# Feed-forward products by Strassen's scheme over pairs of tiles, its sums on GpSimd, in a float32 streaming encoder

## The chip, the cores and the metric

One NeuronCore of a Trainium2 chip runs the program. The metric is device microseconds (us) of one execution; a lower number is better. TensorE is PE in the rows below, VectorE DVE, ScalarE ACT, GpSimd POOL, and SyncE, which issues most transfers, SP.

## What is computed

A trunk of two layers over 528 tokens (16 meta tokens and 512 frames) with 1024 features: first a multi-scale retention layer, then a layer of latent attention; each ends with a dense feed-forward network (FFN) of hidden width 2816. Cut to what matters here:

```python
def swiglu(hn, w1, w3, w2):
    return (jax.nn.silu(hn @ w1) * (hn @ w3)) @ w2

for layer in range(2):
    h = h + mixer(rmsnorm(h, norm_mix_g[layer]))
    h = h + swiglu(rmsnorm(h, norm_ffn_g[layer]), ffn_w1[layer], ffn_w3[layer], ffn_w2[layer])
return rmsnorm(h, final_g)[:, 128:]
```

In the first layer the FFN runs over all 528 tokens, in the second over the 512 frames alone. Inputs, weights and result are float32.

## The kernel before, in words

Activations are held transposed: features on 128 partitions, tokens along the free axis. `self.h` is the residual stream, eight tiles of 128 x 528. TensorE multiplies in fp32r, a shorter float, so each float32 operand is split exactly into a head and a rest (`split`, lines 210 to 213: ACT copies the head with a cast, DVE subtracts it to get the rest), and a product is three passes: head by head, head by rest, rest by head (`mm`, line 239).

`gemm` (line 250) runs over the tiles of 128 output columns. For each it loads the weight column (128 x 1024 in the FFN's up direction), splits it whole, runs the passes over the eight tiles of the contraction, and calls an `evac`. For 528 tokens a pass is two instructions of 264 columns (line 246), for 512 frames one of 512 (line 248).

`ffn` (line 619) works in two parts, each half of the hidden width: 22 column tiles of w1 and w3 in turn (11 of each), whose results DVE scales by the norm and multiplies (with a Silu on ACT between) and splits into a hidden tile, and then w2's eight column tiles over these 11 hidden tiles, added to `h`. In layer 0, `prep` (here `prep_mla`, line 351) follows each addition to `h[k]` in the second part: it makes the split operands of the next stage while TensorE is at the next column. In the same way the last retention projection makes the FFN's operands (`prep_ffn`, line 616), and so does the last attention projection (line 769). Layer 1's second half of w2 runs through `finish` (line 869): it does 256 frames, then the other 256, with weights kept, so that the first half's final norm and output lie under the second half's products.

Order and buffers: the tile framework allots tiles from pools that are open for the whole program: 57 slots of 128 x 528, three weight tiles of 128 x 1024 each for raw, head and rest, and four PSUM tiles of two banks. It orders each engine's instructions, and puts a wait wherever a tile is not ready or not yet free. Each engine works through its own queue strictly in order; so does SP, which issues the weight loads. GpSimd does no arithmetic, only some transfers.

Of the kernel before, what the change touches and what calls it, by code (L numbers as in the profile page):

```python
# [19 lines left out]
P = 128  # L20
# [22 lines left out]
SLOTS = 57  # L43
# [4 lines left out]
# Steps of other work at five places of each head's attention.  # L48
# [33 lines left out]
class Head:  # L82
    """One head's attention over tiles of 128 queries, in stages."""
# [37 lines left out]
    def weights(self, i):  # L121
        """The probabilities with keys on partitions, split."""
        k, nc, p = self.k, self.nc, self.p[i]
        qs = slice(i * P, (i + 1) * P)
        if i == 0:
            self.ph = k.tp.tile([P, 4, SEQ], F32R, tag="pth", name=k.name("pth"), bufs=1)
            self.pl = k.tp.tile([P, 4, SEQ], F32R, tag="ptl", name=k.name("ptl"), bufs=1)
            for z in (self.ph, self.pl):
                nc.vector.memset(z.bitcast(F32)[:, 3, 256:384], 0.0)
# [5 lines left out]
        k.split(self.ph[:, : i + 1, qs], self.pl[:, : i + 1, qs], ptv)  # L135
        k.stacked(self.pm[:, qs], pt[:META, 512 : 512 + P], 64)

    def values(self):
# [15 lines left out]
class Kernel:  # L154
    """Activations are kept transposed, features on partitions and tokens (16 meta tokens, then
    512 frames) along the free axis. A float32 product is three float32r passes over operands
    split exactly into a 12-bit head and a 12-bit rest."""

    def __init__(self, ctx, tc, a):
# [15 lines left out]
    def slot(self, dtype=F32):  # L175
        return self.sp.tile([P, T], dtype, tag="slot", name=self.name("s"))

    def temp(self):
        return self.tp.tile([P, T], F32, tag="tmp", name=self.name("t"))

# [91 lines left out]
    def square_add(self, acc, x, first):  # L272
        """acc += x * x"""
# [730 lines left out]
```

## Time and profile before

| | |
|---|---|
| median of 3 runs (lowest to highest) | 1505.89 us (1505.42 to 1507.55) |
| span of the profiled execution | 1505.8 us |
| PE busy | 1486.9 us, 99% |
| DVE busy | 846.7 us, 56% |
| ACT busy | 571.0 us, 38% |
| POOL busy | 20.9 us, 1% |
| matrix instructions | 10450 |
| transfers | 133.91 MB, mean 89 GB/s |

The page gives the profiled execution's span, from its first to its last instruction; its time as a whole stands in no row, and the span lies 0.1 us under the median of the runs. A matrix instruction's listed duration overlaps the next one's, so its price in a stream is read from the chain, as the time of a stretch over its count. Rows of the trace show the form as partitions x elements, then how many there are, the busy time and the mean in ns.

### The profile page before, as it was taken

To read this page: it belongs to the slowest core of one execution; us is meant where nothing else is said; L and a number is where in the kernel's file an instruction comes from. 1 tells how busy PE (TensorE), PEld (TensorE's weight loads), DVE (VectorE), ACT (ScalarE), POOL (GpSimd) and SP (SyncE) were. 2 spreads that over 40 slices of the span, in tenths; PEclk is the share of its full clock that TensorE was granted. 3 is DMA by queue.
4 is the path that set the end of the run, shared out by engine and by line. 5 is a ranking of instruction groups with operands and counts; after the bars stand their busy time and mean duration, and the time that the engine had idled before them with its cause. 6 is when DMAs were issued, how large, how long until landed. Compare 5 with 4: busy or idle time off the path is not lost.

```text
span 1505.8 us, 24568 instructions
## 1 busy us (share of the span) xinstructions
PE 1486.9 (99%) x10450; PEld 1392.0 (92%) x10450; DVE 846.7 (56%) x1286; ACT 571.0 (38%) x946; POOL 20.9 (1%) x44
## 2 busy tenths in 40 slices
PE   8999999999999999999999999999999999999997
PEld 8999999999999999999999998889888888888896
DVE  7665565565577444234445667677885443344464
ACT  5452342342345222123224435666464222222251
POOL 1000000000000000000000000110000000000000
PEclk9999999999999999999999999999999999999998
DMA  5213213213212222332323422321113223323251
GB/s 202 88 47 111 80 46 110 80 48 109 70 58 94 89 88 70 96 112 86 95 67 87 139 84 80 103 67 67 57 44 111 98 81 88 112 98 98 81 160 57
DMA packets 43022, 133.91 MB, mean 89 GB/s; under 512 B 5136, under 2 KB 8720, under 8 KB 42912
## 3 DMA queue, kind: packets, MB, share of 16 engines
q1 hardware_dynamic: 40464, 125.98, 25.7%
q0 software_dynamic: 2448, 6.36, 1.5%
q8 instruction: 82, 1.34, 0.4%
q14 instruction: 28, 0.23, 0.0%
HBM read 128.91 MB, written 2.10 MB: 87 GB/s over the span
## 4 chain that ended last, share of the span: by engine, by line
PE 96%; DVE 1%; ACT 1%; DMA 0%; issue 0%; SPq 0%; DVEq 0%; ACTq 0%
PE ps L246 47%; PE ps L248 28%; PE ps L483 7%; PE ps L915 4%; PE ps L566 2%; PE ps L106 2%; PE ps L524 2%; PE ps L147 1%; PE ps L489 1%; PE ps L491 1%; PE ps L132 1%; PE ps L296 1%; DVE s L208 1%; ACT s L864 0%; DMA s<-w_q 0%; PE ps L567 0%
## 5 line engine op out<-in xcount | busy, mean ns | idle before, releaser
L246 PE MATMUL ps<-s,whi 128*128 128x264 f32 x3904 | 638.2, 285 | 6.5 <-ACT s L224 6.4
L246 PEld LDWEIGHTS ps<-s,whi 128*128 128x128 f32 x3904 | 543.4, 189 | 8.0 <-ACT s L224 6.8
L212 ACT CAST whi<-raw 128x1024 fp32r<-128x1024 f32 (+5 forms) x270 | 246.1, 917 | 652.3 <-PE ps L246 310.2
L246 PE MATMUL ps<-s,wlo 128*128 128x264 f32 x1952 | 398.4, 286 | 0.0
L248 PE MATMUL ps<-s,whi 128*128 128x512 f32 x1248 | 391.9, 395 | 0.5 <-DVE s L208 0.4
L208 DVE TENSOR_TENSOR wlo<-raw,whi 128x1024 fp32r<-128x1024 f32 (+5 forms) x270 | 284.3, 1056 | 107.2 <-ACT whi L212 104.7
L246 PEld LDWEIGHTS ps<-s,wlo 128*128 128x128 f32 x1952 | 303.8, 189 | 0.0
L248 PEld LDWEIGHTS ps<-s,whi 128*128 128x128 f32 x1248 | 232.4, 188 | 54.0 <-DVE s L208 1.0
L248 PE MATMUL ps<-s,wlo 128*128 128x512 f32 x624 | 244.8, 392 | 0.0
L208 DVE TENSOR_TENSOR t<-ps,s 128x528 f32<-128x528 f32 (+1 forms) x120 | 83.0, 700 | 279.8 <-PE ps L246 162.0
L248 PEld LDWEIGHTS ps<-s,wlo 128*128 128x128 f32 x624 | 117.1, 188 | 27.0
L208 DVE TENSOR_TENSOR h<-ps,h 128x528 f32<-128x528 f32 (+2 forms) x100 | 64.9, 653 | 93.3 <-PE ps L246 64.3
L483 PE MATMUL ps<-whi,s 128*128 128x256 f32 x640 | 116.0, 281 | 0.0
L208 DVE TENSOR_TENSOR s<-ps,s 128x256 fp32r<-128x256 f32 (+4 forms) x107 | 59.4, 571 | 89.9 <-ACT s L212 51.5
L483 PEld LDWEIGHTS ps<-whi,s 128*128 128x128 f32 x640 | 99.2, 189 | 0.2
L483 PE MATMUL ps<-wlo,s 128*128 128x256 f32 x320 | 89.7, 280 | 0.0
L483 PEld LDWEIGHTS ps<-wlo,s 128*128 128x128 f32 x320 | 60.4, 189 | 0.0
L212 ACT CAST s<-t 128x528 fp32r<-128x528 f32 (+2 forms) x68 | 40.2, 603 | 48.2 <-DVE t L208 39.4
L208 DVE TENSOR_TENSOR s<-s,s 128x528 fp32r<-128x528 f32 (+4 forms) x85 | 53.7, 657 | 4.9 <-ACT s L212 4.7
L212 ACT CAST s<-ps 128x256 fp32r<-128x256 f32 (+2 forms) x72 | 31.7, 445 | 61.0 <-PE ps L483 50.1
L208 DVE TENSOR_TENSOR s<-t,s 128x528 fp32r<-128x528 f32 (+2 forms) x68 | 44.5, 664 | 8.6 <-ACT s L212 8.4
L212 ACT CAST s<-s 128x528 fp32r<-128x528 f32 (+2 forms) x57 | 32.8, 584 | 39.8 <-DVE s L208 37.3
(140 smaller groups left out, 1105.1 us busy)
## 6 DMA issues: line engine op xcount, KB each, us to landing
raw<-w SPq DMA_DIRECT2D x99, 512.0 KB, 3.5
raw<-w SPq DMA_DIRECT2D x24, 384.0 KB, 3.1
raw<-w_v SPq DMA_DIRECT2D x16, 512.0 KB, 3.8
raw<-w_g SPq DMA_DIRECT2D x16, 512.0 KB, 3.4
raw<-w_ro SPq DMA_DIRECT2D x16, 512.0 KB, 3.4
raw<-w SPq DMA_DIRECT2D x24, 320.0 KB, 2.9
raw<-w_mo SPq DMA_DIRECT2D x8, 512.0 KB, 3.4
raw<-w_q SPq DMA_DIRECT2D x7, 512.0 KB, 4.2
```

What stands on the lines that cost most here:

```text
L106: nc.tensor.matmul(out, x[:, qs], y[:, cs], start=t == 0, stop=t == 4 and not masked)
L132: nc.tensor.transpose(pt[:, j * P : (j + 1) * P], p[:, META + j * P : META + (j + 1) * P], k.ident)
L147: nc.tensor.matmul(po[:, q0:SEQ], x, y, start=j == 0 and t == 0, stop=False)
L208: self.nc.vector.tensor_tensor(out=out, in0=a, in1=b, op=op)
L212: self.nc.scalar.copy(out=hi, in_=src)
L246: mm(ps[:, h * 512 : h * 512 + HT], w[p], x[q][:, h * HT : (h + 1) * HT], start=s, stop=e)
L248: mm(ps[:, :SEQ], w[p], x[q], start=s, stop=e)
L296: self.nc.tensor.matmul(ps[:, h * 512 : h * 512 + w], one, z[:, h * w : (h + 1) * w], start=i == 0, stop=i == len(acc) - 1)
L483: mm(ps[:, :256], x[k][p][:, c], w[k][q], start=k == 0 and i == 0, stop=k == last and i == 2)
L524: nc.tensor.matmul(ps[:n, half * 512 : half * 512 + HT], k[d][p][:, t0 : t0 + n], q[d][s][:, half * HT : (half + 1) * HT], start=i == 0, s ...
L566: mm(out, v[j][p][:, c], s[:, c0 : c0 + HT], start=j == 0 and i == 0, stop=False)
L915: nc.tensor.matmul(ps[:, :n], p, q, start=k == 0 and i == 0, stop=k == len(x) - 1 and i == 2)
```

## The change

Two column tiles and two halves of the tokens make a 2 x 2 block product, and each needs seven products in place of eight. In the up direction a block is one tile of w1 beside the same tile of w3, and contraction tiles are taken in pairs; in the down direction it is two column tiles of w2. The weights come in as four quarters; `factors` makes seven factors of them, four by a sum on GpSimd, and splits each of the seven. `operands` does the same for the activations, once for each pair of tiles: four sums on GpSimd and seven split operands, kept in one tile of 7 x 2 x 264. `quad` runs the seven products into four banks and combines them on DVE. The hidden product Silu(a) * b goes to GpSimd as well. w2 is taken in four parts (3, 3, 3 and 2 pairs of hidden tiles), and the second FFN has no `finish`.

Pools are opened and shut by stage: 45 slots for retention, none in the FFN, 53 for the attention layer; the FFN has PSUM as eight single banks. Weight heads and rests are now tiles of 512 columns. The next stage's operands are made after the FFN (`mla` begins with `prep_mla` for all eight tiles) and, for the second FFN, after the attention layer is through.

```diff
+PARTS = (3, 3, 3, 2)
     def weights(self, src, n=WC):
-        raw, hi, lo = self.weight_tiles()
+        raw, hi, lo = self.weight_tiles(n)
         self.nc.sync.dma_start(out=raw[:, :n], in_=src)
-        self.split(hi[:, :n], lo[:, :n], raw[:, :n])
+        for c0 in range(0, n, WP):
+            c = slice(c0, min(n, c0 + WP))
+            self.split(hi[:, c], lo[:, c], raw[:, c])
         return hi, lo
...
     def prep_ffn(self, layer, k):
...
+        self.nc.scalar.activation(out=self.vv[:, k % 2], in_=v, func=AF.Copy, scale=self.g(f"ffn{layer}", k))
+        self.square_add(self.acc[:, :n], v, k == 0)
+        if k % 2:
+            self.x.append(self.operands(self.xp, self.vv, n // 2))
...
+    def operands(self, pool, vv, w):
...
+        add(out=tm[:, 2], in0=b12, in1=b11, op=ALU.subtract)
+        add(out=tm[:, 0], in0=b12, in1=b22, op=ALU.subtract)
+        add(out=tm[:, 1], in0=b22, in1=tm[:, 2], op=ALU.subtract)
+        add(out=tm[:, 3], in0=b21, in1=tm[:, 1], op=ALU.subtract)
+        self.split(xp[:, 0:2, 0, :w], xp[:, 0:2, 1, :w], vv[:, :, :w])
+        self.split(xp[:, 3:7, 0, :w], xp[:, 3:7, 1, :w], tm)
+        self.split_scaled(xp[:, 2, 0, :w], xp[:, 2, 1, :w], b22, -1.0)
+        return xp
+    def factors(self, src, n):
...
+        nc.sync.dma_start(out=s3, in_=src[:, 3 * n : 4 * n])
+        nc.sync.dma_start(out=raw[:, : 3 * n], in_=src[:, : 3 * n])
+        a11, a12, a22 = (raw[:, i * n : (i + 1) * n] for i in range(3))
+        nc.gpsimd.tensor_tensor(out=s1, in0=s3, in1=a22, op=ALU.add)
+        nc.gpsimd.tensor_tensor(out=s3, in0=s3, in1=a11, op=ALU.add)
+        for j, z in enumerate((a11, s3, s2, s1, a12, a22, s2)):
+            if j == 2:
+                nc.gpsimd.tensor_tensor(out=s2, in0=s1, in1=a11, op=ALU.add)
+            if j == 6:
+                nc.gpsimd.tensor_tensor(out=s2, in0=s2, in1=a12, op=ALU.add)
+            hi, lo = (t[:, :n] for t in self.ring())
+            self.split(hi, lo, z)
+            yield hi, lo
+    def quad(self, src, xs, w):
...
+                for i, (p, q) in enumerate(((0, 0), (0, 1), (1, 0))):
+                    nc.tensor.matmul(bank[:, :w], wt[p][:, c], xp[:, j, q, :w], start=first and k == 0 and i == 0,
+                                     stop=last and k == len(xs) - 1 and i == 2, skip_group_check=True)
+        a, b, c, d = (self.bank() for _ in range(4))
+        product(a, 0, True, False)
+        nc.scalar.copy(out=q1, in_=a[:, :w])
+        product(d, 3, True, False)
+        product(b, 4, True, True)
+        self.tt(u2, b[:, :w], q1, ALU.subtract)
+        self.tt(u3, d[:, :w], u2, ALU.add)
+        product(c, 5, True, False)
+        c2 = self.temp()[:, : 2 * w]
+        self.tt(c2[:, w:], c[:, :w], u3, ALU.add)
+        product(a, 1, False, True)
+        product(d, 6, False, True)
+        self.tt(c2[:, :w], d[:, :w], u2, ALU.add)
+        product(c, 2, False, True)
+        self.tt(u3, c[:, :w], u2, ALU.add)
+        return a[:, :w], u3, c2
+        def up(m):
+            c11, c12, c2 = self.quad(a[f"w13_{layer}"][m], x, w)
...
+            self.tt(c1[:, :w], c11, r[:, :w], ALU.mult)
+            nc.vector.scalar_tensor_tensor(out=c1[:, w:], in0=c12, scalar=-1.0, in1=r[:, w:n], op0=ALU.mult, op1=ALU.mult)
+            self.tt(c2, c2, r[:, :n], ALU.mult)
+            nc.scalar.activation(out=c1, in_=c1, func=AF.Silu)
...
+            nc.gpsimd.tensor_tensor(out=vv[:, m % 2], in0=c1, in1=c2, op=ALU.mult)
+            if m % 2:
+                hid.append(self.operands(self.hp, vv, w))
+        def down(part, xs, last):
+            for q in range(KD // 2):
+                c11, c12, c2 = self.quad(a[f"w2_{layer}_{part}"][q], xs, w)
...
+                self.tt(h1[:, :w], c11, h1[:, :w], ALU.add)
+                self.tt(h1[:, w:], h1[:, w:], c12, ALU.subtract)
+                self.tt(h2, h2, c2, ALU.add)
+                if last and not full:
+                    for m in (2 * q, 2 * q + 1):
+                        self.square_add(acc, self.h[m][:, META:], m == 0)
     def mla(self):
+        for k in range(KD):
+            self.prep_mla(k)
```

What the change makes of the order is shown at three places. The first is POOL's queue in the first FFN's up direction, at a steady place. L731, L732, L735 and L737 are the four sums of one block's weights (`s1`, `s3`, `s2`, `s2` again), L805 is the hidden product, L714 to L716 are sums of `operands`. Before, this queue had nothing here.

```order
L731 TENSOR_TENSOR s1_1199_7716<-s3_1201_7718,raw_1198_7715 128x512
L732 TENSOR_TENSOR s3_1201_7718<-s3_1201_7718,raw_1198_7715 128x512
L805 TENSOR_TENSOR e_1139_7415<-t_1164_7551,t_1157_7498 128x528
L714 TENSOR_TENSOR e_1166_7558<-e_1139_7415 128x264
L715 TENSOR_TENSOR e_1166_7558<-e_1139_7415,e_1166_7558 128x264
L716 TENSOR_TENSOR e_1166_7558<-e_1139_7415,e_1166_7558 128x264
L735 TENSOR_TENSOR s2_1200_7717<-s1_1199_7716,raw_1198_7715 128x512
L737 TENSOR_TENSOR s2_1200_7717<-s2_1200_7717,raw_1198_7715 128x512
L731 TENSOR_TENSOR s1_1226_7868<-s3_1228_7870,raw_1225_7867 128x512
```

The weights' sums of a block (`raw_1198`) stand around the hidden product of the block two before it (`t_1164`).

The second is DVE's queue at the same place. L245 with `wlo` is the rest of a weight factor, with `bk` the combining of a bank, with `xp` the rest of activation operands; L800 is one of the scalings by the norm.

```order
L245 TENSOR_TENSOR e_1140_7417<-bk_1143_7420,e_1140_7417 128x264
L245 TENSOR_TENSOR wlo_1186_7653<-raw_1172_7574,whi_1185_7652 128x512
L800 SCALAR_TENSOR_TENSOR t_1164_7551<-e_1140_7417,r_83 128x264
L245 TENSOR_TENSOR wlo_1188_7669<-raw_1172_7574,whi_1187_7668 128x512
L245 TENSOR_TENSOR wlo_1190_7687<-s2_1174_7576,whi_1189_7686 128x512
L245 TENSOR_TENSOR xp_1165_7557<-e_1139_7415,xp_1165_7557 128x2x264
L262 SCALAR_TENSOR_TENSOR xp_1165_7557<-e_1139_7415,xp_1165_7557 128x264
L245 TENSOR_TENSOR e_1167_7569<-bk_1169_7571,e_1167_7569 128x264
L245 TENSOR_TENSOR xp_1165_7557<-e_1166_7558,xp_1165_7557 128x4x264
```

The rests of the hidden operands (`xp`) now stand between a block's last weight rests and the combining of its first banks (`e_1167`), and take what POOL wrote (`e_1139`, `e_1166`).

The third is DVE's queue where the first FFN ends. Before, with L225 the operands of the next stage and L208 on `h0` and `h1` the additions of w2's product:

```order
L208 TENSOR_TENSOR h0_73<-ps_994_8629,h0_73 128x528
L208 TENSOR_TENSOR wlo_1021_8813<-raw_1019_8811,whi_1020_8812 128x768
L225 SCALAR_TENSOR_TENSOR s_1003_8711<-h0_73,gains_81,s_1002_8710 128x528
L225 SCALAR_TENSOR_TENSOR s_1005_8716<-h0_73,gains_81,s_1004_8715 128x512
L208 TENSOR_TENSOR wlo_1024_8855<-raw_1022_8853,whi_1023_8854 128x640
L208 TENSOR_TENSOR h1_74<-ps_1006_8719,h1_74 128x528
```

And now:

```order
L245 TENSOR_TENSOR h7_71<-h7_71,t_1766_10598 128x528
L245 TENSOR_TENSOR h6_70<-h6_70,e_1749_10541 128x264
L409 MEMSET meta_v0_1775_10645 80x512
L409 MEMSET meta_v1_1776_10646 80x512
L409 MEMSET meta_p0_1777_10647 80x528
L409 MEMSET meta_p1_1778_10648 80x528
L409 MEMSET xm_1779_10649 128x192
L262 SCALAR_TENSOR_TENSOR s_1783_10662<-h0_64,gains_72,s_1782_10661 128x528
L245 TENSOR_TENSOR acc_82<-acc_82,t_1788_10674 128x528
L262 SCALAR_TENSOR_TENSOR s_1785_10667<-h0_64,gains_72,s_1784_10666 128x512
```

The next stage's operands for all eight tiles stood between the products' additions; now they stand behind the last of them.

## Rows read from the trace of the kernel before

**Rows 1.** The page: busy time by engine, and the chain that ended last.
```profile
PE 1486.9 (99%) x10450; PEld 1392.0 (92%) x10450; DVE 846.7 (56%) x1286; ACT 571.0 (38%) x946; POOL 20.9 (1%) x44
PE 96%; DVE 1%; ACT 1%; DMA 0%; issue 0%; SPq 0%; DVEq 0%; ACTq 0%
```

**Rows 2.** The chain in order of time: start us, length us, what, count.
```profile
478.19 381.59 PE ps L246 x3120
...
859.78 0.49 PE ps L296 x4
...
1137.54 294.04 PE ps L248 x1272
1431.57 38.90 PE ps L915 x330
```

**Rows 3.** Windows, first FFN's second part (720 to 860) and second FFN (1180 to 1330).
```profile
720.00:780.00 60.00, 60.00 (x491) 60.00 (x491) 26.75 (x32) 16.18 (x20) 0.00 (x0) 1.00 0.26 81
...
780.00:860.00 80.00, 80.00 (x659) 80.00 (x658) 41.76 (x56) 32.67 (x47) 1.62 (x3) 1.00 0.35 109
...
1180.00:1330.00 150.00, 150.00 (x651) 121.84 (x650) 59.89 (x72) 38.64 (x48) 0.00 (x0) 1.00 0.30 95
```

**Rows 4.** Groups by form, DVE with two operands: count, busy us, mean ns, idle before.
```profile
L208 DVE TENSOR_TENSOR wlo<-raw,whi 128x1024 fp32r<-128x1024 f32 x176 | 214.8, 1221 | 44.2 <-ACT whi L212 41.8
L208 DVE TENSOR_TENSOR wlo<-raw,whi 128x768 fp32r<-128x768 f32 x36 | 34.5, 958 | 6.0 <-ACT whi L212 6.0
L208 DVE TENSOR_TENSOR wlo<-raw,whi 128x512 fp32r<-128x512 f32 x12 | 8.0, 686 | 1.7 <-ACT whi L212 1.7
L208 DVE TENSOR_TENSOR wlo<-raw,whi 128x384 fp32r<-128x384 f32 x6 | 3.3, 556 | 4.1 <-ACT whi L212 4.0
L208 DVE TENSOR_TENSOR t<-t,t 128x528 f32<-128x528 f32 x34 | 24.0, 705 | 2.6 <-ACT whi L212 0.5
L208 DVE TENSOR_TENSOR t<-ps,s 128x512 f32<-128x512 f32 x44 | 30.2, 691 | 117.8 <-PE ps L248 117.7
L208 DVE TENSOR_TENSOR h<-ps,h 128x256 f32<-128x256 f32 x16 | 6.7, 420 | 10.7 <-PE ps L915 10.6
L225 DVE SCALAR_TENSOR_TENSOR s<-h,gains,s 128x528 fp32r<-128x528 f32 x24 | 18.3, 761 | 2.1 <-ACT s L224 2.1
L225 DVE SCALAR_TENSOR_TENSOR s<-h,gains,s 128x512 fp32r<-128x512 f32 x16 | 11.9, 746 | 0.4 <-ACT s L224 0.4
L886 DVE SCALAR_TENSOR_TENSOR h<-h,gains,s 128x256 f32<-128x256 f32 x16 | 6.5, 478 | 0.0
```

**Rows 5.** Groups by form: the slowest per element on DVE, DVE's clearing, POOL's only arithmetic-like row.
```profile
L308 DVE RECIPROCAL s<-s 128x512 f32<-128x512 f32 x2 | 6.7, 3348 | 0.8 <-ACT s L306 0.8
...
L326 DVE MEMSET meta_p<- 80x528 f32 x2 | 1.0, 498 | 0.1
...
L994 POOL MEMSET const-float32-0.0<- 128x1 f32 x1 | 0.1, 98 | 0.2 <-issue 0.2
```

**Rows 6.** Groups by form, ACT.
```profile
L212 ACT CAST whi<-raw 128x1024 fp32r<-128x1024 f32 x176 | 184.6, 1050 | 481.7 <-PE ps L246 236.2 <-issue 140.4 <-PE ps L248 99.3
L224 ACT ACTIVATE s<-h,gains 128x528 fp32r<-128x528 f32 x24 | 17.6, 732 | 5.7 <-DVE h L208 4.3 <-DMA h<-xT 0.8
L638 ACT ACTIVATE t<-t 128x528 f32<-128x528 f32 x22 | 14.0, 643 | 0.4 <-DVE t L208 0.4
L212 ACT CAST whi<-raw 128x512 fp32r<-128x512 f32 x12 | 6.8, 618 | 10.7 <-PE ps L248 4.0 <-issue 4.0 <-DMA raw<-w 1.6
```

**Rows 7.** Timeline, the end: start us, length us, engine, what, idle before.
```profile
1494.29 0.42 DVE L208 TENSOR_TENSOR h<-ps,h 128x256 f32<-128x256 f32 x1 [2.47 <-PE ps L915]
...
1495.73 0.70 PE L881 MATMUL ps<-s,ones 128*128 128x256 f32 x2 [1.48 <-DVE s L208]
1496.47 0.47 ACT L882 ACTIVATE s<-ps,eps_rms 128x256 f32<-128x256 f32 x1 [1.25 <-PE ps L881]
1496.98 1.75 DVE L883 RECIPROCAL s<-s 128x256 f32<-128x256 f32 x1 [1.30 <-ACT s L882]
1498.77 3.25 DVE L886 SCALAR_TENSOR_TENSOR h<-h,gains,s 128x256 f32<-128x256 f32 x8
1499.28 3.78 SPq L888 DMA_DIRECT2D outT<-h  x8
```

**Rows 8.** The page's part 6: a weight load, KB, us to landing.
```profile
raw<-w SPq DMA_DIRECT2D x99, 512.0 KB, 3.5
```

More of the change, by code (lines that the diff above doesn't have):

```diff
@@ L55, in drain, with __init__, __getitem__ @@
         pass
+class Pieces:
+    def __init__(self, tiles):
+        self.tiles = tiles
+    def __getitem__(self, key):
+        rows, c = key
+        i = c.start // WP
+        return self.tiles[i][rows, c.start - i * WP : c.stop - i * WP]
 class Filler:
@@ L172, in name, with pool, shut, slot @@
         return f"{s}_{self.n}"
-    def slot(self, dtype=F32):
-        return self.sp.tile([P, T], dtype, tag="slot", name=self.name("s"))
+    def pool(self, name, side="left", bufs=1, space=None):
+        kw = {"space": space} if space else {}
+        self.n += 1
+        c = self.tc.tile_pool(name=f"{name}{self.n}", bufs=bufs, side=side, reuse_waits="tile", **kw)
+        self.open[name] = c
+        return c.__enter__()
+    def shut(self, *names):
+        for n in names:
+            self.open.pop(n).__exit__(None, None, None)
+    def slot(self, dtype=F32, pool=None):
+        return (pool or self.sp).tile([P, T], dtype, tag="slot", name=self.name("s"))
     def temp(self):
         return self.tp.tile([P, T], F32, tag="tmp", name=self.name("t"))
+    def wide(self, dtype=F32):
+        return self.tp.tile([P, EW], dtype, tag="wide", name=self.name("e"))
+    def bank(self):
+        return self.pp.tile([P, 512], F32, tag="bk", name=self.name("bk"))
     def ps(self):
@@ L393, in retention @@
         next(values)
-        self.xm = self.meta_tiles(x, "xm")
+        self.meta_tiles(x)
         r = self.slot()
@@ L617, in ret_project @@
                 yield
-    def ffn(self, layer, full, prep):
+    def operands(self, pool, vv, w):
+        nc = self.nc
+        add = nc.gpsimd.tensor_tensor
+        xp = pool.tile([P, 7, 2, HT], F32R, tag="xp", name=self.name("xp"))
+        tm = self.wide()[:, : 4 * w].rearrange("p (j c) -> p j c", j=4)
+        (b11, b12), (b21, b22) = ((vv[:, i, :w], vv[:, i, w : 2 * w]) for i in range(2))
+        add(out=tm[:, 2], in0=b12, in1=b11, op=ALU.subtract)
[6 more added lines that the diff above has]
+        return xp
@@ new lines, in quad, with product @@
+    def quad(self, src, xs, w):
+        nc = self.nc
+        n = len(xs) * P
+        fac = self.factors(src, n)
+        ev = self.wide()[:, : 4 * w].rearrange("p (j c) -> p j c", j=4)
+        q1, u2, u3 = ev[:, 0], ev[:, 1], ev[:, 2]
+        def product(bank, j, first, last):
+            wt = next(fac)
+            for k, xp in enumerate(xs):
+                c = slice(k * P, (k + 1) * P)
+                for i, (p, q) in enumerate(((0, 0), (0, 1), (1, 0))):
[17 more added lines that the diff above has]
+        return a[:, :w], u3, c2
@@ L644, in add @@
-        def add(m, ps):
-            hv = self.two(self.h[m]) if full else self.h[m][:, META:]
-            self.tt(hv, self.view(ps, full), hv, ALU.add)
-            if part:
-                prep(m)
-        for part in range(2):
-            hid.clear()
-            up = self.gemm(a[f"w13_{layer}"], part * KH, KH, x, full, evac=evac,
-                           mid=None if part else partial(self.rstd, r, acc, D, self.eps_rms[:, 0:1], full),
-                           mid_at=1)
-            drain(up)
-            if part and not prep:
-                self.finish(a[f"w2_{layer}"][part], hid)
-            else:
-                drain(self.gemm(a[f"w2_{layer}"][part], 0, KD, list(hid), full, chunk_k=6, evac=add))
+        vv = None
@@ new lines, in ffn @@
+        m = 0
+        for part, size in enumerate(PARTS):
+            end = 2 * sum(PARTS[: part + 1])
+            ahead = 1 if part < len(PARTS) - 1 else 0
+            while m < end + ahead:
+                up(m)
+                m += 1
+            xs, hid[:] = hid[:size], hid[size:]
+            last = part == len(PARTS) - 1
+            if last:
+                self.shut("xp")
+            down(part, xs, last)
+        if not full:
+            rstd()
+            for k in range(KD):
+                hv = self.h[k][:, META:]
+                nc.vector.scalar_tensor_tensor(out=hv, in0=hv, scalar=self.g("final", k), in1=r[:, :n],
+                                               op0=ALU.mult, op1=ALU.mult)
+                nc.sync.dma_start(out=a["outT"][:, k], in_=hv)
@@ L971, in _arrays @@
     for n in range(2):
[L972 to L974 removed]
+        w1, w3, w2 = i["ffn_w1"][n], i["ffn_w3"][n], i["ffn_w2"][n]
+        cols = lambda z, m: z[:, m * P : (m + 1) * P]
+        a[f"w13_{n}"] = np.stack([_pair(cols(w1, m), cols(w3, m)) for m in range(KH)])
+        k = 0
+        for part, size in enumerate(PARTS):
+            rows = w2[k : k + 2 * size * P]
+            k += 2 * size * P
+            a[f"w2_{n}_{part}"] = np.stack([_pair(cols(rows, m), cols(rows, m + 1)) for m in range(0, KD, 2)])
     wk = i["mla_w_kv_a"]
```

215 lines of the change are left out of this document (104 added, 111 removed).

## The prediction

> **What bounds the kernel now.** I read the page's shares first: PE is busy for 99% of the span, the chain that ended last is 96% PE, DVE has 56%, ACT 38%, and POOL does nothing that counts [rows 1]. The chain in order of time then gives prices in a stream: after the norm's short product comes one unbroken stretch of 3120 instructions of 264 columns in 381.59 us, 0.1223 us each; in the second FFN 1272 of 512 columns take 294.04 us, 0.2312 each; and in `finish` 330 of 256 columns take 38.90 us, 0.1179 each [rows 2]. The windows show why nothing else matters there: PE is busy for the whole of each stretch at a granted clock of 1.00 (its upper level, 2.4 GHz), while DVE has 60 of 150 us in the second FFN, and 42 of 80 where the first FFN also makes the next stage's operands [rows 3]. So fewer columns are worth their full price, as long as the engines that feed PE keep up.
>
> **What PE saves.** Before, the first FFN issues 44 x 8 x 3 x 2 + 8 x 22 x 3 x 2 = 3168 instructions of 264 columns: 387.4 us. Now 22 up blocks of 7 x 4 x 3 = 84 and 16 down blocks (twelve of 63, four of 42) make 2772 of the same width: 339.0 us, so -48.4. The second FFN has 1320 of 512 and 528 of 256 columns before, 305.2 + 62.3 = 367.4 us; now 2772 of 256, 326.8 us, so -40.6. Together **-89 us** if PE never waits.
>
> **What DVE and POOL have to do for it.** An up block of the first FFN takes PE 84 x 0.1223 = 10.27 us (before, 96: 11.74). DVE, from the rows by form [rows 4]: seven rests of 512 at 0.686, 4.80; five bank combinations at 0.42, 2.10; the scalings 0.42 + 0.48 + 0.70, 1.60; and every second block the activation rests, 0.70 + 1.22 + 0.48, so 1.20 a block. That is 9.70 us, 94% of PE's time (97% in the second FFN, whose block takes PE 9.90 us), where DVE had 40 to 52% [rows 3]. ACT's seven casts of 0.618, its Silu of 0.643 and the rest come to some 6.5 us [rows 6]; they hide. The weights are the same bytes a block as before, and a load of 3.5 us [rows 8] has one block of lead.
>
> POOL gets four sums of 512, one product of 528, and two sums of 264 a block. No row shows a two-operand sum there: its only arithmetic-like row is a one-element clearing of 98 ns [rows 5]. From below, DVE's own 0.686 us for 512 bounds it; from above, DVE's slowest row, a reciprocal of 512, 3.35 us [rows 4, 5]. A sum is nearest to the first; I take 1.22 us, DVE's row of 1024 elements, as of an engine that fetches its two operands one after the other, and 0.70 (the 528 row) for 264. POOL then has 4.88 + 1.22 + 1.40 = 7.50 us a block, 73% of PE's time.
>
> The Trainium skill's GPSIMD Engine Reference (section 3.1) puts a two-operand add of 2048 elements at 4497 ns against 2293 ns for DVE; by that ratio, an estimate, 512 would take 1.34 us, and POOL 8.2 us a block. No run here shows it.
>
> **Whether the two run side by side** decides the sign. DVE's rows don't change with company: 0.686 us with both operands in SBUF, 0.691 with one in PSUM, under PE, ACT and transfers at work [rows 4]. But POOL is the one engine that has not been at work beside it. The slack is small: DVE has 0.57 us a block, and the gain that is left after the costs below, some 50 us over 76 blocks, is 0.66 more. If over 1.2 of POOL's 7.50 us hold DVE up, a sixth, the change loses. With so much from SBUF on both engines I hold it likelier than not that more than a sixth does.
>
> So the forecast has them share. Of DVE's work, 7.18 us a block has both operands in SBUF (4.80 + 0.48 + 0.70 + 1.20). Taking turns for whole instructions costs 7.18 + 7.50 = 14.68 us a block. If only the streaming is exclusive (1.045 ns an element, from 1.221 - 0.686 us over 512; the fixed parts overlap), it is 5300 elements on DVE and two times 3104 on POOL, 12.03 us. I take the middle, 13.36: no row says which. Against 11.74 before that is +1.62 x 22 = +36 us (+6 to +65). In the second FFN 13.2 (11.9 to 14.55) against 48 x 0.2312 = 11.10: +46 (+18 to +76). A down block of three hidden pairs has seven rests of 384 at 0.556, two additions to `h` from SBUF (0.42 + 0.70), and four sums at 0.958 (the 768 row): 8.8 in turns, 6.9 by streaming, and PE's own 7.70 in the first FFN is the floor; middle 7.8. One of two pairs: 5.8 (5.1 to 6.8), in the second FFN 7.0 with two square sums. First FFN 12 x 7.8 + 4 x 5.8 = 117 against 1056 x 0.1223 = 129: -12 (-16 to +4). Second: 122 against 264 x 0.2312 + 62.3 = 123: -2 (-10 to +15). Sum **+68 us** (-3 to +159).
>
> By the Trainium skill's page SBUF — State Buffer (section "Who interferes with whom") a DVE instruction with two SBUF inputs and a GpSimd instruction that reads SBUF share an interface, and the one that issues second waits for the other's end: it speaks against this change. By that rule the upper sums hold; no run of the kernel before shows it, as POOL reads nothing there.
>
> **What the stages lose at their ends.** Before, all four were under products.
> - First FFN's start: behind the last addition to `h7` stand, behind its own 0.70, 0.73 (scaling), four POOL sums of 0.70, a cast of 1.05 and a rest of 1.22 before the second product can end, 6.5 us, or 7.7 with the weight sum between them in POOL's queue; PE has 2.6 us of other work. +5.
> - First FFN to attention: DVE's queue has, behind the last product, three additions (1.5 us), five clearings (2.2; 0.498 the largest) [rows 5], eight operands of 0.761, seven of 0.746, seven square sums of 0.70 and seven weight rests of 0.686, 24.7 us in all and some 23 back to back. PE needs the last of the eight for its first column and has 5.9 us to do meanwhile: +17. Before, PE went on without a gap (381.59 us to 859.78, then the norm's 0.49) [rows 2].
> - Attention to second FFN: ACT's queue has 16 casts, scalings and squares (0.4 to 1.05 each, 10.9 us) before the fourth operand tile's first factor, and 2.2 more for the rest; PE has 2.5: +11.
> - The end: no first half to hide the norm. Before, 11.5 us from the last product's end to the span's [rows 7]. Now: additions 1.5, a square 0.64 and its sum 0.69, the norm's product and two roots 1.6, the reciprocal 3.35 (1.75 before), eight scalings of 512 in 5.5 (of 256, 3.25), and 3.8 to the end as before: 17.1. +6.
>
> Sum +39. The split of weights into halves and fewer slots (45 and 53 for 57) I cost at nothing: DVE has half its time free there; if slots run out, a wait for the oldest would add a few us a head, which I leave to the range.
>
> The total is +68 + 39 = +107 us on the span of 1505.8, which stands 0.1 us under the median: **1613 us**, 1542 to 1704 by the bounds.
>
> **Rivals.**
> 1. *They run freely, and it is faster.* Place: the up blocks; the price is PE's saving in full. For it: DVE's rows don't heed PE, ACT or transfers, and POOL's chain from L805 to L732 (2.1 + 1.22 + 1.2 + 1.3 for cast and rest between L735 and L737, + 3.7) is 9.5 of 10.3 us. Against: DVE at 94 to 97% with an in-order queue. It decides as soon as under a sixth of POOL's time holds DVE up: 1505.8 - 89 + 39 = 1456 (1440 to 1475). A POOL sum near its lower bound gives nearly the same even with sharing.
> 2. *Whole turns.* The upper sums, 1505.8 + 159 + 39 = 1704, where each instruction on one engine waits for the whole of the other's. For it: both queues would always have the next one ready; against it: the fixed part of a DVE instruction overlaps the next one's already, eight scalings of 0.478 take 3.25 us [rows 4, 7]. The rule of the Trainium skill's page SBUF — State Buffer, quoted above, gives this case.
> 3. *POOL alone is too slow.* No sharing, but a sum takes about 2.3 us, between the bounds: 13.9 us a block on POOL's queue, +47, +62 and down blocks at PE's pace, -27: 1505.8 + 82 + 39 = 1627.
> 4. *The change doesn't do what it says.* The built program has 2772 products of 264 and 2772 of 256 columns in the FFNs, so this is closed.
>
> **How the numbers follow.** Sharing, 0.45; whole turns, 0.12; POOL too slow, 0.08; free, 0.32; a mix that ends within 0.2% (3 us, about what a measurement of this kernel can tell from no change), 0.03. So slower 0.65, faster 0.32, same 0.03. The likeliest case by itself is 1542 to 1704. With both signs open the range must reach from the free case's middle to whole turns: 1448 to 1705, which leaves out about a third of rival 1's lower part and half of rival 2.
>
> **What would show it.** Right: in the up blocks PE's chain is broken by waits for DVE and POOL, a block takes 12 to 14.7 us, a DVE rest of 512 has a mean well over 0.686 us or idles behind POOL, and POOL's sums stretch where DVE runs; gaps of 10 to 17 us on PE at the two stage borders. Wrong: PE's FFN stretches stay 99% busy with blocks of 10.3 and 9.9 us, DVE's 512 rows stay at 0.69; or POOL's rows are long even where DVE is idle (rival 3).

## The result, and the profile after

The changed kernel takes **1760.1 us** (median of 4 runs, 1759.0 to 1764.2) against 1505.8 before: **1.169 times** as long (95% interval 1.1675 to 1.1708), 254 us more. The profiled execution has a span of 1757.2 us.

The page of the changed kernel, shares and slices:

```profile
PE 1494.7 (85%) x10980; PEld 1427.3 (81%) x10980; DVE 1384.0 (79%) x2217; ACT 778.0 (44%) x1539; POOL 597.1 (34%) x512
...
PE   8999999999778878787885999899687777887875
...
PEclk9999999999889999999988999999889999998988
...
PE 59%; DVE 19%; POOL 8%; issue 7%; ACT 5%; DMA 2%; DVEq 0%; POOLq 0%; ACTq 0%
```

PE is busy for 85% where it had 99%, and the chain is 59% PE where it was 96% [rows 1]. The two FFNs are the slices where PE has 7 or 8 tenths. What PE waits for there stands in its largest group (count | busy us, mean ns | idle before, and what ended most of it):

```profile
L756 PE MATMUL bk<-xp,whi 128*128 128x264 f32 (+1 forms) x3696 | 738.1, 301 | 205.3 <-DVE e L245 149.2
```

Of the 205 us that PE idles before these products, 149 end with the combining of a bank on DVE. The windows of an up stretch in each FFN (busy time of PE, its weight loads, DVE, ACT and POOL, each with its instructions; then the granted clock, DMA share and GB/s):

```profile
500.00:560.00 60.00, 46.37 (x335) 44.60 (x334) 53.48 (x68) 25.31 (x44) 37.23 (x28) 0.91 0.21 71
1300.00:1360.00 60.00, 46.99 (x342) 45.53 (x341) 51.50 (x67) 23.35 (x41) 38.14 (x30) 0.89 0.21 67
```

DVE has 53 of 60 us, PE 46, at a granted clock of 0.91 and 0.89 in the mean, where it stood at its upper level, 1.00, throughout [rows 3]. The groups of DVE and POOL by form (instructions | busy us, mean ns | idle before):

```profile
L245 DVE TENSOR_TENSOR wlo<-s,whi 128x512 fp32r<-128x512 f32 x176 | 169.4, 964 | 18.8 <-ACT whi L249 18.8
L245 DVE TENSOR_TENSOR e<-bk,e 128x264 f32<-128x264 f32 x114 | 48.1, 422 | 9.1 <-PE bk L756 8.9
L800 DVE SCALAR_TENSOR_TENSOR t<-e,r 128x264 f32<-128x264 f32 x22 | 20.8, 945 | 0.0
...
L732 POOL TENSOR_TENSOR s<-s,raw 128x512 f32<-128x512 f32 x44 | 67.2, 1528 | 3.1
```

A rest of 512 whose sum POOL made has 964 ns where a rest had 686, and the scaling of 264 has 945 [rows 4]; what reads a bank (`e<-bk,e`) has kept its 422. A stretch of both engines in time order shows how (start, duration):

```profile
536.66 0.42 DVE L245 TENSOR_TENSOR e<-bk,e 128x264 f32<-128x264 f32 x1
537.19 0.43 DVE L245 TENSOR_TENSOR t<-bk,e 128x264 f32<-128x264 f32 x1
537.30 1.29 POOL L735 TENSOR_TENSOR s<-s,raw 128x512 f32<-128x512 f32 x1
537.54 1.61 DVE L245 TENSOR_TENSOR wlo<-s,whi 128x512 fp32r<-128x512 f32 x1
539.07 0.42 DVE L245 TENSOR_TENSOR t<-bk,r 128x264 f32<-128x264 f32 x1
539.41 0.67 DVE L245 TENSOR_TENSOR wlo<-s,whi 128x512 fp32r<-128x512 f32 x1
540.01 0.42 DVE L245 TENSOR_TENSOR t<-bk,e 128x264 f32<-128x264 f32 x1
540.16 1.29 POOL L737 TENSOR_TENSOR s<-s,raw 128x512 f32<-128x512 f32 x1 [1.57 <-DVE wlo L245]
540.35 1.65 DVE L245 TENSOR_TENSOR wlo<-s,whi 128x512 fp32r<-128x512 f32 x1
```

POOL's sum begins at 537.30 and ends at 538.59; the rest issued at 537.54 ends at 539.15, 0.56 us after it. The next rest, with POOL idle, takes 0.67. At 540.16 the same again. The bank combinations take 0.42 us beside a sum or not. The whole trace says the same, and more sharply. The 139 bank combinations of the FFNs that began during a sum or a product of POOL took 0.42 us in the median, as the others did. The 164 rests of 512 that began during one ended 0.55 us after it in the median, eight in ten of them between 0.547 and 0.553 (the 332 others took 0.68 in all). The 105 sums of 512 that began during a two-operand instruction of DVE ended 1.15 us after it (1.28 for the 71 others). So whichever comes second waits until the other is through, and only some 0.13 us of its own time run beside it.

Where the 254 us came from, by the first and last FFN instruction in each trace (for the kernel before by counting instructions along its chain [rows 2]); an up or down block is timed from its first product to the next block's first, by its 84, 63 or 42 instructions in the trace. The kernel before has other blocks; its price is that of the same work there, eight products for seven: 96, 72 and 48 instructions of 264 columns, and in the second FFN half as many of 512 (for w2 the mean with those of 256 in `finish`).

| us | before | after | forecast |
|---|---|---|---|
| gap ahead of the first FFN | 0 | 12.4 | +5 |
| first FFN | 388 | 472.2 | 411 |
| - an up block | 11.74 | 14.84 | 13.36 |
| - a down block of 3, of 2 pairs | 8.8, 5.9 | 9.35, 8.35 | 7.8, 5.8 |
| first FFN to second | 272 | 312.6 | +28 |
| second FFN | 368 | 474.8 | 412 |
| - an up block | 11.10 | 14.90 | 13.2 |
| - a down block of 3, of 2 pairs | 8.4, 5.6 | 9.22, 9.10 | 7.8, 7.0 |
| last product to the end | 11.5 | 17.4 | +6 |

The mean of the blocks of two pairs hides one wait: the first of the four takes 13.9 us in the first FFN and 14.1 in the second, the others 5.8 to 8.2, because PE waits there for the last hidden operands.

What ended the gap ahead of the first FFN:

```profile
479.26 0.69 DVE L245 TENSOR_TENSOR h<-ps,h 128x528 f32<-128x528 f32 x1
...
480.10 0.78 PE L756 MATMUL bk<-xp,whi 128*128 128x264 f32 x2 [12.41 <-DVE h L245]
```

### The profile page after: what moved, and what is told of

Read it like the earlier page. It is cut to its first block, busy times and chain, and to the rows that moved or that the text cites. A ratio compares the mean times of both kernels' runs of the same rounds, so it can differ in the third digit from the quotient of the medians.

```text
span 1757.2 us, 28326 instructions
## 1 busy us (share of the span) xinstructions
PE 1494.7 (85%) x10980; PEld 1427.3 (81%) x10980; DVE 1384.0 (79%) x2217; ACT 778.0 (44%) x1539; POOL 597.1 (34%) x512
## 3 DMA queue, kind: packets, MB, share of 16 engines
q8 instruction: 86, 1.41, 0.3%
## 4 chain that ended last, share of the span: by engine, by line
PE 59%; DVE 19%; POOL 8%; issue 7%; ACT 5%; DMA 2%; DVEq 0%; POOLq 0%; ACTq 0%
PE bk L756 22%; PE ps L294 16%; DVE wlo L245 9%; PE ps L296 7%; PE ps L568 6%; DVE e L245 3%; PE ps L651 2%; DVE t L800 2%; POOL e L715 2%; POOL e L805 2%; POOL e L714 2%; ACT xp L249 2%; PE ps L125 1%; DVE h L245 1%; PE ps L609 1%
## 5 line engine op out<-in xcount | busy, mean ns | idle before, releaser
L756 PE MATMUL bk<-xp,whi 128*128 128x264 f32 (+1 forms) x3696 | 738.1, 301 | 205.3 <-DVE e L245 149.2
L756 PEld LDWEIGHTS bk<-xp,whi 128*128 128x128 f32 x3696 | 616.4, 204 | 228.5 <-DVE e L245 163.1
L756 PE MATMUL bk<-xp,wlo 128*128 128x264 f32 (+1 forms) x1848 | 545.8, 297 | 7.8 <-DVE wlo L245 7.7
L245 DVE TENSOR_TENSOR wlo<-raw,whi 128x512 fp32r<-128x512 f32 (+3 forms) x444 | 374.6, 854 | 53.7 <-ACT whi L249 52.9
L756 PEld LDWEIGHTS bk<-xp,wlo 128*128 128x128 f32 x1848 | 373.3, 203 | 11.1 <-DVE wlo L245 11.0
L294 PE MATMUL ps<-s,whi 128*128 128x264 f32 x1792 | 295.0, 286 | 12.0 <-ACT s L261 6.8
L245 DVE TENSOR_TENSOR wlo<-s,whi 128x512 fp32r<-128x512 f32 (+2 forms) x304 | 255.3, 844 | 23.8 <-ACT whi L249 23.1
L294 PEld LDWEIGHTS ps<-s,whi 128*128 128x128 f32 x1792 | 250.1, 190 | 14.6 <-ACT s L261 7.3
L294 PE MATMUL ps<-s,wlo 128*128 128x264 f32 x896 | 183.1, 286 | 10.1 <-DVE wlo L245 10.1
L737 POOL TENSOR_TENSOR s<-s,raw 128x512 f32<-128x512 f32 (+2 forms) x76 | 93.2, 1226 | 229.5 <-DVE wlo L245 212.8
L294 PEld LDWEIGHTS ps<-s,wlo 128*128 128x128 f32 x896 | 139.9, 190 | 10.8 <-DVE wlo L245 10.8
L731 POOL TENSOR_TENSOR s<-s,raw 128x512 f32<-128x512 f32 (+2 forms) x76 | 102.0, 1342 | 72.7 <-DVE wlo L245 39.1
L296 PE MATMUL ps<-s,whi 128*128 128x512 f32 x368 | 117.5, 400 | 1.6 <-DVE s L245 1.6
L735 POOL TENSOR_TENSOR s<-s,raw 128x512 f32<-128x512 f32 (+2 forms) x76 | 92.8, 1222 | 56.8 <-DVE wlo L245 56.8
L245 DVE TENSOR_TENSOR e<-bk,e 128x264 f32<-128x264 f32 (+1 forms) x228 | 95.3, 418 | 17.1 <-PE bk L756 16.2
L245 DVE TENSOR_TENSOR xp<-e,xp 128x528 fp32r<-128x528 f32 (+3 forms) x60 | 68.1, 1137 | 49.3 <-ACT xp L249 47.7
L732 POOL TENSOR_TENSOR s<-s,raw 128x512 f32<-128x512 f32 (+2 forms) x76 | 103.8, 1365 | 5.6
L245 DVE TENSOR_TENSOR s<-ps,s 128x256 fp32r<-128x256 f32 (+4 forms) x96 | 52.5, 557 | 61.4 <-ACT s L249 53.2
```

Of the source, the lines that this page charges most:

```text
L245: self.nc.vector.tensor_tensor(out=out, in0=a, in1=b, op=op)
L294: mm(ps[:, h * 512 : h * 512 + HT], w[p], x[q][:, h * HT : (h + 1) * HT], start=s, stop=e)
L296: mm(ps[:, :SEQ], w[p], x[q], start=s, stop=e)
L731: nc.gpsimd.tensor_tensor(out=s1, in0=s3, in1=a22, op=ALU.add)
L732: nc.gpsimd.tensor_tensor(out=s3, in0=s3, in1=a11, op=ALU.add)
L735: nc.gpsimd.tensor_tensor(out=s2, in0=s1, in1=a11, op=ALU.add)
```

## The experiments

Each kernel stands beside a run of the kernel before (1505.4 to 1505.6 us). Its time is that of one run; most effects are tens of us. The kernel before itself lay between 1505.4 and 1507.6 us, the changed one between 1759.0 and 1764.2, so effects of 7 or 8 us are near what single runs can tell.

**1. Nobody waits for POOL** (`beside`, the kernel before):

```
+        u = self.const([P, 512], name="beside")
+        for _ in range(80): nc.gpsimd.tensor_tensor(out=u, in0=u, in1=u, op=ALU.add)
+        for _ in range(80): nc.gpsimd.tensor_copy(out=u, in_=u)
+        for _ in range(80): nc.gpsimd.memset(u, 0.0)
```

> The kernel before, with work on POOL that nobody waits for: 80 sums of 512 columns with both operands in SBUF, then 80 copies of 512, then 80 clearings of 512, one after the other from the start (one slot of 57 fewer makes room for their tile). Theory (an instruction of DVE with both operands in SBUF and a sum of POOL take whole turns): as long as the sums run, DVE's rests of 512 columns go from 0.686 us to 1.2 to 1.6 in the mean, its instructions with an operand in PSUM stay at 0.69, and the rests are back at 0.69 under the clearings; a sum alone is about 1.3 us, the shortest of them in the changed kernel. Rival (only the streaming is shared): rests of about 1.0 us. Rival (the rows of the changed kernel are long since POOL is slow by itself and DVE waits for its results): rests stay at 0.69 beside the sums. The time moves little in all three, within 1495 to 1525, since DVE has half its time free here.

1540.0 us. DVE by form, from 10 to 120 us (beside the sums) and, last line, from 215 to 235 us (beside clearings):

```profile
L208 DVE TENSOR_TENSOR s<-s,t 128x528 f32<-128x528 f32 x11 | 13.2, 1213 | 0.0
L225 DVE SCALAR_TENSOR_TENSOR s<-h,gains,s 128x528 fp32r<-128x528 f32 x7 | 11.4, 1631 | 0.0
L308 DVE RECIPROCAL s<-s 128x528 f32<-128x528 f32 x1 | 3.5, 3452 | 0.2 <-ACT s L306 0.2
L208 DVE TENSOR_TENSOR t<-ps,s 128x528 f32<-128x528 f32 x5 | 3.3, 695 | 2.8 <-PE ps L246 2.8
...
L208 DVE TENSOR_TENSOR t<-t,s 128x528 f32<-128x528 f32 x2 | 1.4, 708 | 3.5 <-ACT s L581 3.5
```

No instruction waits for POOL here, and yet what reads two operands in SBUF goes from 0.70 to 1.21 and from 0.76 to 1.63 us. An instruction with one PSUM operand (695 ns) or with one operand (3452) takes what it took, and so does everything beside the clearings. The copies, with one operand to read, hold DVE too (operations of 528 at 0.8 to 1.1). No rest of 512 fell beside the sums, so the theory's own row is missing; the products of 528 stand in for it, and those that began during a sum ended 0.56 us after it. That is the theory. Shared streaming alone would have given about 1.0 for a rest, and there are no results to wait for, so both rivals are out. The time was outside what I gave, +35: of the first 110 us, where the sums fell, DVE has 76 us before.

**2. No work on POOL** (`no_sums`; sums and hidden product left out, raw quarters and activations in their places):

```
-        for j, z in enumerate((a11, s3, s2, s1, a12, a22, s2)):
+        for z in (a11, s3, a12, s3, a12, a22, a22):
```

> The changed kernel without any work on POOL: the sums of weights and of activations are left out (raw quarters and the activations themselves stand in their places), and so is the product of the two hidden halves. PE, DVE and ACT have the same instructions on the same shapes. Theory (turns between DVE and POOL are the loss): up blocks of 10.3 and 9.9 us, at PE's pace, DVE's rests of 512 at 0.69 us, and with the stage borders as they are 1470 to 1510 us. Rival (the loss is DVE's queue in its order, with PE waiting for combinations of banks behind rests, whoever makes the sums): blocks stay over 12.5 us, 1600 to 1700. Rival (PE's lower granted clock after each wait is the larger part): between them, 1520 to 1600, with granted clock still under 0.95 in the FFN.

1491.0 us. Its windows in the same two stages:

```profile
500.00:560.00 60.00, 60.00 (x491) 59.69 (x489) 52.43 (x104) 33.57 (x63) 0.00 (x0) 1.00 0.32 103
1300.00:1360.00 60.00, 60.00 (x508) 59.81 (x507) 52.68 (x107) 34.16 (x65) 0.00 (x0) 1.00 0.32 105
```

And its rests of 512:

```profile
L245 DVE TENSOR_TENSOR wlo<-raw,whi 128x512 fp32r<-128x512 f32 x408 | 275.8, 686 | 77.7 <-ACT whi L249 73.5
```

PE is busy throughout at clock 1.00, with DVE at 52 of 60 us and its rests of 512 at 686 ns. Blocks take 10.45 and 10.35 us on average. So POOL's work costs 268 us of span, and the lower clock goes with PE's waits: without them it is 1.00. Without POOL's work the scheme is 14 us ahead of the kernel before.

**3. The same work on POOL, read by nobody** (`unread`; as 2, but POOL does every sum and product):

```
-        for j, z in enumerate((a11, s3, s2, s1, a12, a22, s2)):
+        for j, z in enumerate((a11, a12, a22, a12, a12, a22, a22)):
```

> The changed kernel with the same sums and products on POOL, but nobody reads them: DVE and ACT take raw quarters and the activations instead, so no engine waits for POOL's results. Theory (the turns cost, not the waits for results): 1690 to 1750 us, up blocks of 14 to 15 us, rests of 512 at 0.9 to 1.0. Rival (PE is held by the chain of results through POOL, ACT and DVE): 1480 to 1540.

1751.7 us (1.7 over what I gave), up blocks of 14.42 and 14.43. With no wait for POOL's results the changed kernel's time is 8 us less; that POOL works at all is worth 261.

**4. All of it on DVE** (`sums_dve`; nc.gpsimd.tensor_tensor becomes nc.vector.tensor_tensor):

> The changed kernel with every sum and product of POOL on DVE, nothing on POOL: no turns, but DVE has 9.7 + 4 x 0.686 + 0.70 + 2 x 0.42 = 14.0 us a block of the first FFN, 13.8 in the second; down blocks of three pairs 7 and 4 of 384 columns at 0.556 and the rest, 9.3. Theory: bound by DVE, up blocks of 14.0 to 14.6 us, 1690 to 1730 us, a little faster than the changed kernel, as a sum on DVE takes 0.69 us where POOL takes 1.3 of DVE's time. Rival (the loss is POOL's latency): under 1620. Rival (the loss is DVE's order of work): 1740 to 1800.

1656.6 us, faster by 104 and by more than forecast: up blocks of 12.63 and 12.65 us, not 14.0 to 14.6. DVE's durations overlap by some 0.1 us when they stand back to back, as in the stretch above (539.41, 540.01, 540.35), so a sum of its rows overstates its queue; whether that is all of the difference was not tried.

**5 and 6. Half of POOL's work** (`wsums_out` leaves out the sums of weights as in 2, `acts_out` the work on activations):

> The changed kernel with the four sums of weights a block left out (raw quarters in their places); POOL keeps the sums of activations and the hidden product, and all its results are read. Theory: all of POOL's own time is added to DVE's queue. An up block is the larger of PE's 10.5 us (without work on POOL) and DVE's queue, 14.87 of the changed kernel less POOL's 4 x 1.05 = 10.7; so up blocks of 10.5 to 11.0 us, 1500 to 1530 us with the gap ahead of the first FFN back, as POOL makes the last operands there. Rival (turns cost only where the sums of activations stand between ACT and DVE, one result waiting for another): up blocks over 12.5, 1590 to 1660.

> The changed kernel with POOL's work on activations left out (sums of activations and the hidden product; the activations stand in their places), the four sums of weights a block stay on POOL. Theory: DVE's queue is 14.87 less POOL's 1.08 + 2 x 0.6 = 12.6 us a block, and up blocks take that; down blocks keep all their sums, 9.2 and 7.8; the gap ahead of the first FFN is gone: 1620 to 1665 us. Rival (the chain of activation sums is the loss): up blocks under 11.3, 1500 to 1560.

1584.1 and 1653.9 us. Over the 1491.0 without any that is +93 for the activations and +163 for the weights: 256 of the 269 that both cost. `acts_out` came as expected (blocks of 12.72 and 12.84). `wsums_out` came between theory and rival, and nearer the rival: 12.01 and 12.29. The starts of ACT's Silu from its third block on are 10.2, 13.2, 10.2 and 12.7 us apart. The operands' seven sums and rests come with every second block, which falls behind PE, while the other goes at PE's pace; my average over two blocks had hidden that. Where such a block loses its time (what PE waited for: us, times, longest; then the place in time order):

```profile
PE bk L750 <- DVE e L245: 51.1, 22, 2.7
```
```profile
532.24 1.21 POOL L715 TENSOR_TENSOR e<-e,e 128x264 f32<-128x264 f32 x1
...
533.53 0.82 POOL L716 TENSOR_TENSOR e<-e,e 128x264 f32<-128x264 f32 x1
...
534.38 1.07 ACT L249 CAST xp<-e 128x1056 fp32r<-128x1056 f32 x1 [2.29 <-POOL e L716]
...
535.49 1.26 DVE L245 TENSOR_TENSOR xp<-e,xp 128x1056 fp32r<-128x1056 f32 x1 [1.41 <-ACT xp L249]
...
536.66 0.43 DVE L245 TENSOR_TENSOR e<-bk,e 128x264 f32<-128x264 f32 x1
...
537.14 0.52 PE L750 MATMUL bk<-xp,whi 128*128 128x264 f32 x2 [2.68 <-DVE e L245]
```

POOL's sums come one after the other, ACT casts the last of them, DVE stands idle for 1.41 us until it can make the rest, and the bank that PE needs is combined behind that rest. This is the rival's chain of results, lengthened by turns (1.21 us for a sum that takes 0.73 alone), and PE's 22 waits of this kind are 51 of the 93 us. No run has the activations' work unread without the sums of weights, so the shares of the chain and of the turns stay open here. The first FFN starts 10.7 us late in `wsums_out`, 2.0 in experiment 2, 3.9 in `acts_out` and 13.6 in experiment 3: this gap is POOL's work on the operands, read or not.

**7 and 8. Sums by transfers** (accumulating DMAs issued from POOL; `dma_sums` all four, `dma_two` two, the rest on DVE):

```
+            nc.gpsimd.dma_start(out=z, in_=part[i], accum_op=ALU.add)
```

> The changed kernel with nothing on POOL but the issue of transfers: the four sums of weights are made by transfers that add to their tile (eleven loads of a quarter for the sums, where there was one, beside the three raw quarters), the sums of activations and the hidden product are DVE's. If the transfers keep up, DVE's queue is some 8.4 + 1.4 = 9.8 us, under PE's 10.5, and the time is near that without sums, 1490 to 1520 us. Rival (an adding transfer is slow, four in a row do not land within a block, or PE waits for rests of late sums): over 1600. Rival (an adding transfer or its issue on POOL holds DVE up as POOL's sums do): DVE's rests over 0.8 us.

> As the run with adding transfers, but only the first two sums are made so (three more loads of a quarter); the other two sums, the sums of activations and the hidden product are DVE's. DVE's queue is some 8.4 + 1.4 + 2 x 0.6 = 11.0 us a block: 1515 to 1560 us if the transfers keep up, faster than the version with all sums on DVE (1656.6) in any case where an adding transfer lands within 5 us. Rival: the adding transfers are late, over 1660.

2406.5 and 1731.7 us, the rivals. The issues of `dma_sums` (KB each, median us to landing):

```profile
s<-w POOLq DMA_DIRECT2D x308, 256.0 KB, 6.1
s<-w SPq DMA_DIRECT2D x176, 256.0 KB, 3.7
raw<-w SPq DMA_DIRECT2D x44, 768.0 KB, 7.6
```

The last sum takes four transfers one after the other, 3.7 + 3 x 6.1 = 22 us, and an up block takes 22.4 and 22.6; the tiles have one buffer each. DVE's rests stay at 684 ns, so transfers and their issue do not hold DVE. In `dma_two` an adding transfer lands in 4.5 us in the median, within the 5 that I had named as enough to beat experiment 4, and yet the kernel is 75 us behind it, with 18% of its chain on transfers. A plain load and the adding one stand behind each other there, in tiles of one buffer. With two buffers for the two sums of `dma_two` more might be had; that was not tried, since without any sum the kernel is only 14 us ahead.

**9 and 10. Sums in the kernel before, where DVE has room** (one line in `weights`, for the first FFN's up products; 2 or 4 times a tile):

```
+            self.nc.gpsimd.tensor_tensor(out=self.beside, in0=raw[:, :512], in1=raw[:, 512:], op=ALU.add)
```

> The kernel before, with work on POOL in the up products of the first FFN alone: two sums of 512 columns for each tile of weights, made from the two halves of the raw tile and read by nobody (four for a pair of tiles, as many as the changed kernel has for a block; one slot of 57 fewer). Theory (all of POOL's own time is added to DVE's queue): for a pair of tiles DVE has 26.5 us of 60, so 5.2, and POOL 4 x 1.05 = 4.2; together 9.4, under PE's 11.74: the time stays within 3 us of the 1505.6. Rival (any turn on a weight's rest holds PE up): 1515 to 1540.

> As the run with two sums a tile, with four: POOL 8.4 and DVE 5.2 for a pair of tiles, together 13.6 against PE's 11.74, so 22 x 1.86 = 41 us more: 1535 to 1555 us, with PE waiting for rests of weights. Rival (turns overlap, as the streaming alone is shared): about 11.7 a pair, within 8 us of the kernel before. Rival (POOL's sums have no part in it, the changed kernel's order of work has): no change either.

1512.9 and 1529.6 us: 7 and 24 more, where I had given at most 3 and 41. Two rows of `ffn_two` in time order, then the windows of 520 to 580 us, `ffn_two` and `ffn_four`:

```profile
519.14 1.64 POOL L237 TENSOR_TENSOR beside<-raw 128x512 f32<-128x512 f32 x1
...
519.55 2.31 DVE L208 TENSOR_TENSOR wlo<-raw,whi 128x1024 fp32r<-128x1024 f32 x1
```
```profile
520.00:580.00 60.00, 60.00 (x494) 60.00 (x493) 34.03 (x32) 16.71 (x21) 25.89 (x19) 1.00 0.27 86
```
```profile
520.00:580.00 60.00, 60.00 (x495) 60.00 (x494) 42.40 (x32) 16.73 (x20) 57.33 (x35) 1.00 0.26 89
```

A rest of 1024 doubles (2.31 for 1.22), DVE's busy time rises from 26.5 to 34.0 and 42.4 us, and PE does not notice: with two sums a tile its stretch of 3120 instructions takes 380.5 us (381.6 before). What was lost lies ahead of it: that stretch starts at 482.6 and not 478.2, as the first tiles' sums fall beside the last operands. With four, the +41 in the stream did not come: POOL is full there (57 of 60 us) and falls behind, but only a raw tile's buffer waits for it, and DVE's products of a bank go beside the sums; PE loses its 24 us mostly ahead of the stream (14.6, at 492.8) and around the second half. So DVE's whole queue plus POOL's time, which I had used from experiment 5 on, is too hard a model; only operations with two operands in SBUF take turns. These rows also price a sum whose two operands are different columns: 1.28 to 1.30 us undisturbed (the shortest and the median of the 88 sums of `ffn_two`), where experiment 1's, with the same columns as both operands and as result, had 1.05. The expectations of 5, 6, 9 and 10 used 1.05.

**11. A third of PE's work away** (`two_pass`):

```
-                for i, (p, q) in enumerate(((0, 0), (0, 1), (1, 0))):
+                for i, (p, q) in enumerate(((0, 0), (1, 0))):
```

> The changed kernel with the second of the three passes of each product left out in both FFNs (heads of the weights by rests of the activations): 56 instructions an up block for 84; DVE, ACT and POOL have all they had. Theory (the block is DVE's queue with POOL's turns in it): the time stays over 1700 us, for PE's third is waited away. Rival (PE, at the lower clock that it is granted after each wait, is on the chain for most of a block): a third of its 1284 us of FFN instructions goes, of which at least half counts: under 1580.

1726.8 us, 33 less. Most of the third of PE's work is waited away, at a granted clock of 0.88 in the mean for the changed kernel's 0.94. PE does not set the pace of a block.

## Why the prediction was wrong, point by point

- **Direction and mechanism were right:** 1613 us was slower for the reason given. In the up blocks PE waits for DVE, DVE's rests stretch, and experiments 2 and 3 show that POOL's work alone does it: 1491 without, 1752 with it unread.
- **The step that failed** is "I take the middle, 13.36: no row says which". Whole turns hold, rival 2 of the prediction, as the ends of 164 rests and 105 sums show. I gave that 0.12 against 0.45, on the ground that eight scalings ran closer than their durations; that saves some 0.1 us an instruction, and not the streaming. The middle is 91 of the 147 us between 1613 and 1760, for the prediction's own upper sums come to 1704. A sum was well priced: 1.22 taken, 1.29 measured (0.73 for the shortest of 256 and 264, 0.70 taken). With the measured prices POOL has 4 x 1.29 + 1.33 (a product of 528) + 2 x 0.73 = 7.95 us a block, and 7.18 + 7.95 = 15.1; measured 14.84 and 14.90. That this comes so near is in part luck: turns save some time where they meet, and for 11% of the first up stretch of either FFN, counted in the trace, neither POOL nor a two-operand instruction of DVE is at work. By the same sum experiments 5 and 6 would have 10.0 (PE's own 10.3) and 12.3 us; they have 12.0 to 12.3 and 12.7 to 12.8, for waits come on top. The two up stages are 33 and 37 us above the forecast: 22 x 1.48 and 22 x 1.70.
- **What had spoken for whole turns.** The estimate of 1.34 by the Trainium skill's GPSIMD Engine Reference (section 3.1) was closer to the 1.29 than my 1.22. The rule of the Trainium skill's page SBUF — State Buffer (section "Who interferes with whom") agrees in every part that was run: two SBUF inputs on DVE against a reading instruction on POOL, the second waits for the other's end (0.55 and 1.15 us above), a PSUM operand (0.42) or a clearing (0.71 for 528) is free of it.
- **Down blocks** were forecast at 7.8 with the same middle; whole turns gave 8.8 of the rows alone, and 9.35 and 9.22 were measured. The blocks of two pairs are 8.35 and 9.10 against 5.8 and 7.0, of which the wait of the first for the last hidden operands is the larger part; the prediction has no term for it. Together 29 us in the first FFN (145.6 - 117), 25 in the second (147.0 - 122).
- **Stage ends** came out close, one excepted. First FFN to attention: the first column ends 17.9 us later than its products alone take (17 forecast); PE idles for 14 of them, 9.4 in one wait for DVE's queue of operands and clearings as listed, and the granted clock there is 0.71 in the mean. Attention to second FFN: 12.5 (11). The end: 17.4 (17.1). The start of the first FFN was 12.4 for 5: I counted from the last addition to `h` on and let PE work for 2.6 us meanwhile. PE's wait ends with that addition itself, which began 11.6 us after PE's last product, as DVE's queue has the rests of earlier operands ahead of it and stands idle for 1.76 and 1.73 us until ACT has cast what POOL made of them.
- **Costed at nothing:** of the 40.5 us more between the FFNs, 17.9 + 12.5 are the two borders and some 10 are left. PE's waits inside attention sum to 8.3 us (1.0 before), at the softmax's steps on ACT (`L125 <- ACT t` 2.8, `L168 <- ACT t` 1.9). Whether the changed order of fill-in work, the probabilities split in pairs, or the slots do this was not tried.
- **Rival 1** was priced too low. Free of POOL the kernel has 1491, not 1456: up blocks of 10.45 and 10.35 for 10.27 and 9.90 (the first two of each FFN take 11.0 to 14.0, the later ones 10.2 to 10.5 and 9.9 to 10.1), down blocks at 7.67 and 7.44 for 7.70 and 7.43 but those of two pairs at 6.8 and 7.0 for 5.14 and 4.95, and the borders. **Rival 3** is out: POOL alone needs 8 us a block and idles for over a third of an up stretch. **Rival 4** was closed.

Added up: 33 + 37 + 29 + 25 = 124 us in the blocks, 7 at the start, 10 inside attention, and some 6 in small differences are the 147 us between 1613 and 1760. No complete version here beats the kernel before; the nearest, all sums on DVE, is 151 us behind, and the bound without any sum is 14 ahead.

## What to carry to other kernels

An idle POOL is not free room beside a DVE that reads two operands from SBUF: a POOL sum of 512 (1.29 us) stops such DVE work for as long as it lasts, so moving all of POOL's work to DVE (0.69 us a sum) was faster by 104 us than "taking load off" it. Before giving POOL arithmetic, add its undisturbed time to DVE's two-operand time in each block and compare that sum with the bounding engine. Where it stays under, as in experiment 9, the sums cost nothing in the stream, though they still do at stage ends; where results go from POOL through ACT back into DVE's queue, waits come on top (experiment 5). Average over blocks only what every block does: work that falls on every second one (experiment 5) overruns there and is not paid back in the next.

## What the runs showed of the hardware that I had not expected

A two-operand sum of 512 on POOL takes 1.05 us where both operands and the result are the same columns, and 1.28 to 1.30 where the operands differ (the changed kernel's sum that writes over one of its operands, L732, also has 1.26 at its shortest). A copy on POOL, with one operand, holds DVE as well, a clearing does not. An accumulating transfer of 256 KB took 6.1 us from issue to landing in the median with eleven loads a block, 4.5 with three, against 3.6 to 3.7 for a plain one beside it.
